# A hybrid decoder trunk on one core: the triangular solve of a gated DeltaNet layer is turned back one projection later

## Chip, core and metric

The kernel runs on one core of a Trainium2 chip. The metric is the device time of one execution in microseconds (us), the median of three runs. Five engines work side by side, each through its own instructions in order: TensorE (PE, matmuls and transposes), VectorE (DVE), ScalarE (ACT), GpSimd (POOL) and SyncE (SP, which here only issues DMAs).

## What is computed

Four pre-norm residual layers over 256 tokens of width 1024, in float32: a pooling mixer, a gated DeltaNet mixer (GDN), latent attention (MLA), and a pooling mixer again, then a final norm. Layer by layer it is

```python
h = rmsnorm(x, norm_g[i])
x = x + mixer(h)                     # pool, GDN, MLA, pool
```

The change lies mostly in the GDN layer. For 8 heads it projects `h` to q, k, v and a gate, runs a causal convolution of width 4 and a SiLU over q, k and v, and then needs the inverse of a unit lower triangular matrix per head and chunk:

```python
qkv = jax.nn.silu(causal_depthwise_conv(qkv, conv_w))
L = jnp.where(strict, jnp.einsum('bhnid,bhnjd->bhnij', k_beta, k) * decay, 0.0)
A = jnp.eye(C, dtype=L.dtype) + L
sol = lax.linalg.triangular_solve(A, rhs, left_side=True, lower=True)
```

`decay` is `exp(g_i - g_j)`; q and k are L2-normalised; the state is carried over the chunks, and the result is normalised, gated and projected out.

## The kernel before

**Weights.** Every weight comes as a strip `raw` of float32 (SP issues its DMA, L133). ACT rounds it to `whi` (L149, or L153 with a gain), and DVE takes the rest, `wlo = raw - whi` (L150, L154); for strips whose number stands in the argument `pool`, POOL does it. PE then adds three products per block, hTh·whi, hTl·whi and hTh·wlo (L162). `whi` and `wlo` have rings of 9 buffers, so ACT and DVE can be some strips ahead of PE and no further.

**The GDN layer** is written as a list of steps (the string `order`). `g0` to `g3` project the gate (and end in the SiLU `gsg`, L676); `k0 k1`, `q0 q1` and `v0` to `v2` each project 512 columns, run the convolution (ACT scales the first tap into `cv` or `vc`, L753; DVE adds three more, L756) and the SiLU (`kqT` L798, `vc` L920). k and q then go through PE transposes (L804), squares and sums for the norm (`sq`, `ssq`), and a product with kT (L817); v goes through transposes (L924) and a scaled copy (`vR`, L927). `V3` is the projection of v3 alone, `c3` the rest of it. `d` takes the exponentials of the decays `DT` and `Gb` on ACT (L746); `a0 a1` make the matrices `LT`.

**The solve.** `s` is a substitution over 32x32 blocks: DVE transposes them into `Lb` (L857), POOL runs 31 pairs of a multiplication and a subtraction (L863, L867), and the result is turned back by a DVE transpose (L869) and copied into `T` by ACT (L876) and by POOL (L878). `i` (inverses) joins the blocks to full inverses: transposes into `U` on DVE (L947), then matmuls in pairs (L956). `u0 u1` use them.

**Order.** The program is written straight on, and a scheduler then sorts each engine's instructions by when they can be ready; a `with later(...)` block keeps its instructions behind the ones that it names. Each engine runs its list strictly in that order. The steps stood as `g0 k0 d a0 g1 k1 a1 s q0 v0 v1 i v2 q1 V3 c3 g2 u0 u1 g3`, and turning back (L869 to L878) was the end of `s`, with nothing to hold it back.

**The norm.** `x` has two tiles of 128 tokens. Each finished part of the residual is squared and summed on ACT (`part_done`, L256), the sums are joined on POOL, and the last part reads the square root of what came before as an extra column of `x`, so that the sum over it is whole (L294, L297, L298). `begin` multiplies the first 256 columns of each half by the gain on POOL (`hg`, L385); `rest` raises to the power -1/2 (`xr`, L390) and makes `h` on DVE (L397) and ACT (L402).

Of the kernel before, what the change touches and what calls it, by code (L numbers as in the profile page):

```python
# [16 lines left out]
P = 128  # L17
# [25 lines left out]
def trunk(ctx: ExitStack, tc: tile.TileContext, x, positions, norm_g, pool_w_in, pool_w_grp,  # L43
# [241 lines left out]
    def part_done(t, a, n, apart=False):  # L285
        s = small(f"ms{t}{a // 256}", 1)
        end = a + n == D
        more = int(end and not apart)
        with later(*[m for e, m in mark.items() if e == "rest"]):
            sumsq(xs[t][:, a:a + n + more], n + more, s, scale=float(D) ** -0.5)  # L290
        if a == 0:
            nc.gpsimd.tensor_scalar(s, s, EPS, None, ALU.add)
        elif not more:
            nc.gpsimd.tensor_tensor(out=s, in0=s, in1=ms[t], op=ALU.add)  # L294
        ms[t] = s
        if a and not end:
            nc.gpsimd.tensor_scalar(s, s, float(D), None, ALU.mult)  # L297
            nc.gpsimd.tensor_tensor(out=xs[t][:, D:], in0=s, in1=half, op=ALU.pow)  # L298
# [5 lines left out]
    def load_x(t, c):  # L304
        sl = slice(c * CW, (c + 1) * CW)
        for b in range(2):
            nc.sync.dma_start(out=xs[t][b * 64:(b + 1) * 64, sl], in_=by_row(x, t)[b, :, sl])
# [3 lines left out]
    nc.scalar.dma_start(out=grow, in_=norm_g[0].rearrange("(k p) -> k p", p=P))  # L311
    ones = const.tile([P, P], F32, name="ones")
# [120 lines left out]
    class Final(Normed):  # L433
# [3 lines left out]
        def feed(self, t):  # L437
            y = self.rest(t) if final else [xs[t][:, :CW], xs[t][:, CW:D]]
            for c in range(2):
                sl = slice(c * CW, (c + 1) * CW)  # L440
                for b in range(2):
                    nc.sync.dma_start(out=by_row(out, t)[b, :, sl],
                                      in_=y[c][b * 64:(b + 1) * 64])

    def layer_out(w, yT, ks, i, gain=None):
# [62 lines left out]
    def pool_layer(i, j, hT):  # L508
# [80 lines left out]
        for g in order:  # L589
            gs = gate(g)  # L590
            if not place:
                with later(*[m for k, m in mark.items() if k not in ("rest", "strip")]):
                    turn_params()
                    window_counts()
            elif setups:
                with later(*[m for k, m in mark.items() if k not in ("rest", "strip")]):
                    setups.pop(0)()
# [57 lines left out]
    def gdn_layer(i, j, hT):  # L655
# [23 lines left out]
        order = "g0 k0 d a0 g1 k1 a1 s q0 v0 v1 i v2 q1 V3 c3 g2 u0 u1 g3".split()  # L679
# [63 lines left out]
        def decays():  # L743
            with later(mark["gate"]):
# [3 lines left out]
        def conv(*tiles):  # L748
# [5 lines left out]
            for ps, c, o in tiles:  # L754
                for d in range(1, 4):
                    nc.vector.scalar_tensor_tensor(out=o[:, d:], in0=ps[:, :S - d],  # L756
                                                   scalar=tp(3 - d, c), in1=o[:, d:],
                                                   op0=ALU.mult, op1=ALU.add)
# [4 lines left out]
        solve = big("solve", 2, B, C)  # L763
# [5 lines left out]
        Lg = small("Lg", M, B, bufs=1)  # L769
# [84 lines left out]
        def substitution():  # L854

            Lb = big("Lb", B, B)
            nc.vector.transpose(Lb, Lg.rearrange("p m c -> p c m")[:, :, None, :].to_broadcast(  # L857
                [P, B, 2, M]))
            pr = small("pr", 136, bufs=1)
# [569 lines left out]
```

## Time and profile before

| | |
|---|---|
| median of 3 runs | 821.5 us (821.17 to 821.84) |
| profiled execution | 820.01 us, span of its trace 818.3 us |
| PE busy in the span | 793.2 us, 97% |
| DVE / ACT / POOL busy | 599.4 / 499.8 / 144.9 us |
| HBM read | 136.74 MB |

All times below are counted from the start of the span. A row of the timeline has a start, a duration, the engine, the line, the operation with its output and inputs, and in brackets how long the engine stood idle before it and what ended that. A matmul's duration overlaps its neighbours', so what a matmul costs PE is the distance between two starts.

### The profile page before, as it was taken

What the parts mean: (1) busy time and instruction counts of PE and PEld (TensorE: products, weight loads), DVE (VectorE), ACT (ScalarE), POOL (GpSimd) and SP (SyncE); (2) the same over time, 40 slices, a digit from 0 to 9 for tenths busy, and PEclk for the clock granted to TensorE, in tenths of its full rate; (3) what the DMA queues carried; (4) which work ended last, traced back from release to release, by engine and by line L of the source; (5) the groups of instructions that cost most, each with busy time, mean ns of one, the idle gap of its engine ahead of it and who ended that gap; (6) DMA issues with size and microseconds to landing.
All of it is one profiled execution on the core that took longest, in us unless ns stands there. A gap on an engine that the chain in (4) does not pass through costs nothing.

```text
span 818.3 us, 16144 instructions
## 1 busy us (share of the span) xinstructions
PE 793.2 (97%) x5966; PEld 754.2 (92%) x5966; DVE 599.4 (73%) x1133; ACT 499.8 (61%) x1007; POOL 144.9 (18%) x300
## 2 busy tenths in 40 slices
PE   8999999999999699999999999999999999999996
PEld 7989998989999698888989999999999989999996
DVE  4699987566999586556677659778877668877862
ACT  5666665567967566456565655566565576566662
POOL 2001100234227821022212013000000210000012
PEclk9999999999999989999999999999999999999999
DMA  6765666646555343322557776753542546576562
GB/s 202 221 186 175 204 208 232 205 155 202 186 180 175 111 129 104 129 78 104 180 151 225 213 175 187 209 144 86 183 170 76 183 153 209 192 216 199 198 201 52
DMA packets 106615, 138.85 MB, mean 170 GB/s; under 512 B 19044, under 2 KB 48936, under 8 KB 106536
## 3 DMA queue, kind: packets, MB, share of 16 engines
q1 hardware_dynamic: 104352, 136.60, 54.3%
q0 software_dynamic: 320, 1.06, 0.4%
q8 instruction: 47, 0.77, 0.4%
q10 hardware_dynamic: 1864, 0.17, 0.2%
q14 instruction: 32, 0.26, 0.1%
HBM read 136.74 MB, written 1.06 MB: 168 GB/s over the span
## 4 chain that ended last, share of the span: by engine, by line
PE 83%; POOL 5%; DVE 5%; issue 2%; ACT 2%; DMA 2%; SPq 0%; POOLq 0%; ACTq 0%; DVEq 0%
PE acc L162 67%; PE aux L162 8%; POOL solve L867 2%; POOL pr L863 2%; DVE wlo L150 1%; DVE cv L756 1%; DVE h L397 1%; PE tp L1332 1%; DMA x<-in_x_dram 1%; DMA raw<-in_pool_w_in_dram 1%; ACT whi L149 0%; DMA raw<-in_gdn_w_in_dram 0%; PE aux L974 0%; PE tp L1070 0%; PE aux L817 0%
## 5 line engine op out<-in xcount | busy, mean ns | idle before, releaser
L150 DVE TENSOR_TENSOR wlo<-raw,whi 128x512 fp32r<-128x512 f32 (+1 forms) x372 | 252.1, 702 | 100.6 <-ACT whi L149 98.8
L149 ACT CAST whi<-raw 128x512 fp32r<-128x512 f32 (+1 forms) x380 | 224.7, 617 | 147.0 <-PE acc L162 81.0
L162 PE MATMUL acc<-hTh,whi 128*128 128x256 f32 x832 | 230.2, 277 | 1.2 <-ACT gsg L676 1.2
L162 PE MATMUL acc<-hTl,whi 128*128 128x256 f32 x832 | 230.9, 278 | 0.0
L162 PE MATMUL acc<-hTh,wlo 128*128 128x256 f32 x832 | 229.8, 277 | 0.0
L162 PEld LDWEIGHTS acc<-hTh,whi 128*128 128x128 f32 x832 | 160.6, 193 | 1.6 <-ACT gsg L676 1.4
L162 PEld LDWEIGHTS acc<-hTl,whi 128*128 128x128 f32 x832 | 160.6, 193 | 0.2
L162 PEld LDWEIGHTS acc<-hTh,wlo 128*128 128x128 f32 x832 | 160.4, 193 | 0.2
L162 PE MATMUL acc<-whi,yTh 128*128 128x256 f32 (+1 forms) x384 | 112.3, 315 | 0.0
L162 PE MATMUL acc<-wlo,yTh 128*128 128x256 f32 (+1 forms) x384 | 112.3, 311 | 0.0
L162 PE MATMUL acc<-whi,yTl 128*128 128x256 f32 (+1 forms) x384 | 89.1, 313 | 0.0
L162 PEld LDWEIGHTS acc<-wlo,yTh 128*128 128x128 f32 x384 | 73.2, 191 | 3.1
L162 PEld LDWEIGHTS acc<-whi,yTh 128*128 128x128 f32 x384 | 72.9, 191 | 3.1
L162 PEld LDWEIGHTS acc<-whi,yTl 128*128 128x128 f32 x384 | 63.1, 191 | 3.4
L153 ACT ACTIVATE whi<-raw,colsT 128x512 fp32r<-128x512 f32 x64 | 44.1, 720 | 30.1 <-DMA raw<-in_pool_w_out_dram 16.9
L153 ACT ACTIVATE whi<-raw,gain 128x512 fp32r<-128x512 f32 x64 | 43.8, 720 | 30.6 <-DMA raw<-in_pool_w_in_dram 25.8
L154 DVE SCALAR_TENSOR_TENSOR wlo<-raw,colsT,whi 128x512 fp32r<-128x512 f32 x64 | 47.3, 764 | 19.1 <-ACT whi L153 18.8
L385 POOL TENSOR_TENSOR hg<-x,gain 128x256 f32<-128x256 f32 x16 | 13.8, 872 | 242.6 <-DVE x L450 211.6
L162 PE MATMUL acc<-wlo,hTh 128*128 128x512 f32 (+1 forms) x144 | 54.7, 384 | 1.7 <-DVE wlo L150 1.5
L162 PE MATMUL acc<-whi,hTh 128*128 128x512 f32 (+1 forms) x144 | 53.0, 381 | 0.7 <-ACT hTh L242 0.7
L154 DVE SCALAR_TENSOR_TENSOR wlo<-raw,gain,whi 128x512 fp32r<-128x512 f32 x64 | 46.5, 745 | 9.8 <-ACT whi L153 9.4
L162 PE MATMUL acc<-whi,hTl 128*128 128x512 f32 (+1 forms) x144 | 42.2, 373 | 0.0
(370 smaller groups left out, 1509.9 us busy)
## 6 DMA issues: line engine op xcount, KB each, us to landing
raw<-in_pool_w_in_dram SPq DMA_DIRECT2D x62, 512.0 KB, 4.4
raw<-in_gdn_w_in_dram SPq DMA_DIRECT2D x48, 512.0 KB, 3.9
raw<-in_pool_w_out_dram SPq DMA_DIRECT2D x32, 512.0 KB, 4.3
raw<-in_mla_w_in_dram SPq DMA_DIRECT2D x24, 512.0 KB, 4.5
raw<-in_mla_w_uq_dram SPq DMA_DIRECT2D x36, 256.0 KB, 3.5
raw<-in_pool_w_grp_dram SPq DMA_DIRECT2D x16, 512.0 KB, 4.1
raw<-in_gdn_w_out_dram SPq DMA_DIRECT2D x16, 512.0 KB, 3.4
raw<-in_mla_w_ukv_dram SPq DMA_DIRECT2D x32, 256.0 KB, 3.5
```

The source lines that it names most:

```text
L149: a = nc.scalar.copy(hi, v)
L150: b = e.tensor_tensor(out=lo, in0=v, in1=hi.bitcast(F32), op=ALU.subtract)
L153: a = nc.scalar.activation(hi, v, AF.Copy, scale=g)
L154: b = e.scalar_tensor_tensor(out=lo, in0=v, scalar=g, in1=hi.bitcast(F32), op0=ALU.mult, op1=ALU.subtract)
L162: return nc.tensor.matmul(inorder(o, n), lhsT=lhs, rhs=woven(rhs, n), start=start, stop=stop)
L385: nc.gpsimd.tensor_tensor(out=self.early[t, a], in0=xs[t][:, sl], in1=self.g[:, sl], op=ALU.mult)
L397: nc.vector.scalar_tensor_tensor(out=h[:, cut:], in0=xs[t][:, sl], scalar=r[:, 0:1], in1=self.g[:, sl], op0=ALU.mult, op1=ALU.mult)
L756: nc.vector.scalar_tensor_tensor(out=o[:, d:], in0=ps[:, :S - d], scalar=tp(3 - d, c), in1=o[:, d:], op0=ALU.mult, op1=ALU.add)
L863: nc.gpsimd.tensor_tensor(out=pv, op=ALU.mult, in0=Lb[:, r + 1:, r:r + 1].to_broadcast([P, n, c]), in1=Tb[:, r:r + 1, :c].to_broadcast([P, ...
L867: mark["blocks"] = nc.gpsimd.tensor_tensor(out=tv, in0=tv, in1=pv, op=ALU.subtract).ins
L1332: nc.tensor.transpose(ps[:, a * P:(a + 1) * P], sb[:, a * P:(a + 1) * P], ident)
```

## The change

1. The steps are now `g0 k0 d a0 k1 a1 s g1 q0 v0 v1 v2 b q1 i V3 c3 g2 u0 u1 g3`: the projection `g1` goes from before `k1` to behind the start of the solve, turning back becomes a step `b` of its own behind `v2`, and `i` goes behind `q1`. `b` is kept behind the latest weight strip and the latest convolution.
2. The solve's buffers are no tiles of their own now: `Lb` lies in `U[0]`, the solution in `U[1]`, `Lg` and the products in the first `X1`. The two small operations on `rki` and `neG` stay in `s`; the multiplication of `ktok` goes with `b`.
3. The multiplication of `Gb` with q (`ev`) goes from POOL to DVE, out of the block that kept it behind the solve; POOL takes the strips (0, 4), none, (3, 7), (3, 7) of the four gate projections, where it took (0, 4), (7), none, (7).
4. The first `x` loads (columns 0 to 511) have their second half of the tokens issued by ACT, and those of tile 1 are issued right behind tile 0's; the last stores of tile 1 likewise go half by ACT.
5. In the norm, a factor D is folded into the scale of the sum, so the scalar multiplication at L297 goes; `hg` of the second half is put behind the power that follows.

```diff
-            sumsq(xs[t][:, a:a + n + more], n + more, s, scale=float(D) ** -0.5)
+            sumsq(xs[t][:, a:a + n + more], n + more, s, scale=unit ** 0.5)
...
-            nc.gpsimd.tensor_scalar(s, s, float(D), None, ALU.mult)
-            nc.gpsimd.tensor_tensor(out=xs[t][:, D:], in0=s, in1=half, op=ALU.pow)
+            mark["sofar"] = nc.gpsimd.tensor_tensor(out=xs[t][:, D:], in0=s, in1=half,
+                                                    op=ALU.pow).ins
...
-        for b in range(2):
-            nc.sync.dma_start(out=xs[t][b * 64:(b + 1) * 64, sl], in_=by_row(x, t)[b, :, sl])
+        for b, queue in enumerate((nc.sync, nc.scalar if c == 0 else nc.sync)):
+            queue.dma_start(out=xs[t][b * 64:(b + 1) * 64, sl], in_=by_row(x, t)[b, :, sl])
...
-                for b in range(2):
-                    nc.sync.dma_start(out=by_row(out, t)[b, :, sl],
-                                      in_=y[c][b * 64:(b + 1) * 64])
+                for b, queue in enumerate((nc.sync, nc.scalar if t else nc.sync)):
+                    queue.dma_start(out=by_row(out, t)[b, :, sl], in_=y[c][b * 64:(b + 1) * 64])
...
             if c == 0:
-                nxt.begin(t, CW)
+                with later(mark.pop("sofar")):
+                    nxt.begin(t, CW)
...
-                            pool=((0, 4), (7,), (), (7,))[vi])
+                            pool=((0, 4), (), (3, 7), (3, 7))[vi])
...
-        order = "g0 k0 d a0 g1 k1 a1 s q0 v0 v1 i v2 q1 V3 c3 g2 u0 u1 g3".split()
+        order = "g0 k0 d a0 k1 a1 s g1 q0 v0 v1 v2 b q1 i V3 c3 g2 u0 u1 g3".split()
...
-        solve = big("solve", 2, B, C)
+        U = [big("U", H, P) for _ in range(NT)]
+        Lb = U[0].rearrange("p m c -> p (m c)").rearrange("p (a b) -> p a b", a=B)
+        solve = U[1].rearrange("p m c -> p (m c)").rearrange("p (n a b) -> p n a b", n=2, a=B)
...
+            nc.vector.reciprocal(rki, rk)
+            nc.vector.tensor_scalar(neG, eG[:, 1, :], -1.0, None, ALU.mult)
+
+        def blocks_back():
+
             nc.vector.transpose(turned_.rearrange("p r c -> p (r c)"),
                                 Tb.rearrange("p r c -> p c r"))
...
+            nc.vector.tensor_tensor(out=ev, in0=ev, in1=qT[hf][:, :, P:], op=ALU.mult)
             with later(mark["blocks"]):
-                nc.gpsimd.tensor_tensor(out=ev, in0=ev, in1=qT[hf][:, :, P:], op=ALU.mult)
...
-            if name == "i":
-
-                with later(mark["strip"], mark["dve"]):
-                    inverses()
+            if name in "bi":
+
+                with later(mark["strip"], mark["dve" if name == "i" else "conv"]):
+                    once[name]()
...
-    load_x(1, 0)
```

How the lists of the engines change at three places; a row is one instruction, or several alike with their count.

ACT's list where step `k0` ends, before: the SiLU of k0 (`kqT`), the exponentials of the decays (`DT`, `Gb`), and the squares and copies of k0.

```order
L798 ACT_TABLE_LOAD
L798 ACTIVATE kqT<-cv 128x256 x4
L149 CAST whi<-raw 128x512
L746 ACT_TABLE_LOAD
L746 ACTIVATE DT<-DT 128x1024
L149 CAST whi<-raw 128x512 x2
L807 ACTIVATE sq<-tp 128x512
L810 COPY ktok<-tp 128x256
L807 ACTIVATE sq<-tp 128x512
L810 COPY ktok<-tp 128x256
L746 ACTIVATE DT<-DT 128x1024
L746 ACTIVATE Gb<-Gb 128x1024
```

The same place on ACT in the changed kernel (its lines are some numbers higher).

```order
L804 ACT_TABLE_LOAD
L804 ACTIVATE kqT<-cv 128x256 x3
L748 ACT_TABLE_LOAD
L748 ACTIVATE DT<-DT 128x1024
L149 CAST whi<-raw 128x512
L804 ACT_TABLE_LOAD
L804 ACTIVATE kqT<-cv 128x256
L149 CAST whi<-raw 128x512 x2
L748 ACT_TABLE_LOAD
L748 ACTIVATE DT<-DT 128x1024
L748 ACTIVATE Gb<-Gb 128x1024
L813 ACTIVATE sq<-tp 128x512
```

The first exponential now stands between the third and the fourth SiLU, with two more table loads around it, and the squares stand behind all three exponentials.

DVE's list where the solve is turned back, before: convolutions of v1 (`vc`), then the transpose, then the last convolutions of v1 and strips.

```order
L150 TENSOR_TENSOR wlo<-raw,whi 128x512
L756 SCALAR_TENSOR_TENSOR vc<-acc,tap,vc 128x254
L869 STREAM_TRANSPOSE solve<-solve 128x512
L756 SCALAR_TENSOR_TENSOR vc<-acc,tap,vc 128x253
L150 TENSOR_TENSOR wlo<-raw,whi 128x512
L756 SCALAR_TENSOR_TENSOR vc<-acc,tap,vc 128x253
L150 TENSOR_TENSOR wlo<-raw,whi 128x512 x3
L756 SCALAR_TENSOR_TENSOR cv<-acc,tap,cv 128x255
```

The same place on DVE in the changed kernel: the `vc` ahead of the transpose are now those of v2, and the `cv` behind it those of q1.

```order
L758 SCALAR_TENSOR_TENSOR vc<-acc,tap,vc 128x254
L150 TENSOR_TENSOR wlo<-raw,whi 128x512
L758 SCALAR_TENSOR_TENSOR vc<-acc,tap,vc 128x253
L878 STREAM_TRANSPOSE U<-U 128x512
L758 SCALAR_TENSOR_TENSOR cv<-acc,tap,cv 128x255
L150 TENSOR_TENSOR wlo<-raw,whi 128x512 x2
L758 SCALAR_TENSOR_TENSOR cv<-acc,tap,cv 128x254
L758 SCALAR_TENSOR_TENSOR cv<-acc,tap,cv 128x253
L758 SCALAR_TENSOR_TENSOR cv<-acc,tap,cv 128x255
```

The transpose moved behind the last convolution of one more projection; what stands right behind it is q1's.

ACT's list at the copies out of the turned solution, before: the copies into `T`, and behind them the SiLU of v1.

```order
L927 ACTIVATE vR<-tp,rki 128x256 x4
L149 CAST whi<-raw 128x512 x2
L876 COPY T<-solve 32x16x32 x2
L920 ACTIVATE vc<-vc 128x512
L149 CAST whi<-raw 128x512
L920 ACTIVATE vc<-vc 128x512
```

And in the changed kernel.

```order
L927 ACTIVATE vc<-vc 128x512
L755 ACTIVATE cv<-acc,tap 128x256 x2
L149 CAST whi<-raw 128x512 x2
L927 ACTIVATE vc<-vc 128x512
L885 COPY T<-U 32x16x32 x2
L934 ACTIVATE vR<-tp,rki 128x256 x2
L755 ACTIVATE cv<-acc,tap 128x256
L149 CAST whi<-raw 128x512 x2
L804 ACTIVATE kqT<-cv 128x256
```

No SiLU of a v projection stands behind the copies now; the next thing of PE's that depends on a row behind them is the convolution and the SiLU of q1.

More of the change, by code (lines that the diff above doesn't have):

```diff
@@ L288, in part_done @@
         more = int(end and not apart)
+        unit = 1.0 / D if end or apart else 1.0
         with later(*[m for e, m in mark.items() if e == "rest"]):
-            sumsq(xs[t][:, a:a + n + more], n + more, s, scale=float(D) ** -0.5)
+            sumsq(xs[t][:, a:a + n + more], n + more, s, scale=unit ** 0.5)
         if a == 0:
-            nc.gpsimd.tensor_scalar(s, s, EPS, None, ALU.add)
+            nc.gpsimd.tensor_scalar(s, s, EPS * D * unit, None, ALU.add)
         elif not more:
@@ L591, in pool_layer @@
             if not place:
-                with later(*[m for k, m in mark.items() if k not in ("rest", "strip")]):
+                with later(*[m for k, m in mark.items() if k not in ("rest", "strip", "conv")]):
                     turn_params()
@@ L595, in pool_layer @@
             elif setups:
-                with later(*[m for k, m in mark.items() if k not in ("rest", "strip")]):
+                with later(*[m for k, m in mark.items() if k not in ("rest", "strip", "conv")]):
                     setups.pop(0)()
@@ L743, in decays @@
         def decays():
-            with later(mark["gate"]):
+            with later(*[m for n, m in mark.items() if n == "gate"]):
                 for a in (*DT, Eb, eG):
@@ L755, in conv @@
                 for d in range(1, 4):
[L756 to L758 removed]
+                    mark["conv"] = nc.vector.scalar_tensor_tensor(
+                        out=o[:, d:], in0=ps[:, :S - d], scalar=tp(3 - d, c), in1=o[:, d:],
+                        op0=ALU.mult, op1=ALU.add).ins
         Q, B = 4, 32
         C = B // 2
[L763 removed]
+        U = [big("U", H, P) for _ in range(NT)]
+        Lb = U[0].rearrange("p m c -> p (m c)").rearrange("p (a b) -> p a b", a=B)
+        solve = U[1].rearrange("p m c -> p (m c)").rearrange("p (n a b) -> p n a b", n=2, a=B)
         Tb, turned_ = solve[:, 0], solve[:, 1]
@@ L768, in gdn_layer @@
                                   which[:, a, :C])
-        Lg = small("Lg", M, B, bufs=1)
+        X1 = [big("X1", H, P)]
+        LX = X1[0].rearrange("p m c -> p (m c)")
+        Lg = LX[:, :M * B].rearrange("p (m c) -> p m c", m=M)
         Ts = big("T", NT, H, P)
@@ L854, in substitution @@
         def substitution():
-            Lb = big("Lb", B, B)
             nc.vector.transpose(Lb, Lg.rearrange("p m c -> p c m")[:, :, None, :].to_broadcast(
                 [P, B, 2, M]))
-            pr = small("pr", 136, bufs=1)
+            pr = LX[:, M * B:]
             for r in range(B - 1):
@@ L932, in values @@
             values_done(vi)
-        U = []
         u1 = []
         def inverses():
-            U.extend(big("U", H, P) for _ in range(NT))
-            X1 = [big("X1", H, P) for _ in range(NT)]
+            X1.append(big("X1", H, P))
             for t in range(NT):
@@ L1006, in gdn_layer @@
                  "c": values_done}
-        once = {"s": substitution, "d": decays, "i": inverses}
+        once = {"s": substitution, "d": decays, "b": blocks_back, "i": inverses}
         for name in order:
-            if name == "i":
-                with later(mark["strip"], mark["dve"]):
-                    inverses()
+            if name in "bi":
+                with later(mark["strip"], mark["dve" if name == "i" else "conv"]):
+                    once[name]()
             elif name in once:
```

5 lines of the change are left out of this document (2 added, 3 removed).

## The prediction

> **What bounds the kernel now.** I read the page first (busy shares), then the list of PE's waits, then the timeline around the longest of them.
>
> ```profile
> PE 793.2 (97%) x5966; PEld 754.2 (92%) x5966; DVE 599.4 (73%) x1133; ACT 499.8 (61%) x1007; POOL 144.9 (18%) x300
> ...
> PE tp L924 <- ACT vc L920: 7.8, 1, 7.8
> PE tp L359 <- DMA x<-in_x_dram: 2.6, 2, 2.2
> ...
> PE acc L162 <- DVE wlo L150: 1.5, 3, 0.8
> PE acc L162 <- ACT gsg L676: 1.2, 1, 1.2
> ```
>
> PE is busy 793.2 of 818.3 us, so at most 25.1 us can come from its idle time. One wait, 7.8 us long, holds a third of that: PE wants to transpose v1's `vc` and ACT has not written it. The timeline says why. The rows are of ACT, DVE, POOL and PE.
>
> ```profile
> 284.01 2.14 ACT L876 COPY T<-solve 32x512 f32<-32x512 f32 x2 [9.08 <-DVE solve L869]
> 286.18 0.63 ACT L920 ACTIVATE vc<-vc 128x512 f32<-128x512 f32 x1
> ...
> 274.45 0.47 DVE L756 SCALAR_TENSOR_TENSOR vc<-acc,tap,vc 128x254 f32<-128x254 f32 x1
> 282.94 1.04 DVE L869 STREAM_TRANSPOSE solve<-solve 128x512 f32<-128x512 f32 x1 [8.01 <-POOL solve L867]
> ...
> 282.68 0.22 POOL L867 TENSOR_TENSOR solve<-solve,pr 128x16 f32<-128x16 f32 x1
> 282.86 1.27 POOL L896 TENSOR_TENSOR Gb<-Gb,kqT 128x512 f32<-128x512 f32 x1
> ...
> 286.42 2.55 POOL L878 COPY T<-solve 32x512 f32<-32x512 f32 x2
> ...
> 286.86 1.11 PE L924 MATMUL tp<-ident,vc 128*128 128x128 f32 x4 [7.79 <-ACT vc L920]
> ...
> 293.02 1.90 PE L956 MATMUL aux<-T,LT 128*128 128x64 f32 x16
> ```
>
> Read upwards: PE waits for a SiLU that waits in ACT's list behind the copies into `T`; these wait for DVE's transpose, which has stood 8.01 us, since 274.92, for POOL's substitution. v1's last convolutions are queued behind that transpose. It is an order problem, not a shortage of any engine. The gap costs more than its length; the table by stretches (PE's count of matmuls in it, then its granted clock) shows what follows:
>
> ```profile
> 240.00:270.00 30.00, 30.00 (x272) 30.00 (x271) 30.00 (x63) 23.12 (x50) 21.14 (x40) 1.00 0.61 178
> ...
> 287.00:292.00 5.00, 5.00 (x24) 5.00 (x25) 4.30 (x6) 5.00 (x13) 2.92 (x5) 0.50 0.61 161
> 292.00:293.00 1.00, 1.00 (x8) 1.00 (x7) 1.00 (x2) 0.78 (x2) 0.00 (x0) 0.66 0.64 246
> ```
>
> The columns behind the length are PE, PEld, DVE, ACT and POOL. At full clock PE starts 272 matmuls in 30 us, 0.110 us each. Right after the gap the clock is 0.50 and 24 take 5.00 us where 2.65 would do, then 8 take 1.00 where 0.88 would do: 2.5 us more. The gap's price is 7.79 + 2.5 = **10.3 us**.
>
> **The change, part by part.**
>
> *Turning back one projection later: -10.3.* A projection of a v is 96 matmuls, 96 x 0.110 = 10.6 us. Before the transpose DVE's list now holds v2's convolutions as well, so DVE gets there some 10.6 us later than 274.9, at about 285.5. When does the substitution end? POOL finished it at 282.90. Its start can move: `g1` is now behind it, which takes 10.6 us of PE's work from ahead of it, but what starts it is DVE, and DVE is 30.00 of 30.00 us busy in the stretch above, so it works off a backlog; I take 1.5 us earlier of the possible 10. Its length can grow: all 31 pairs ran from 247.7 on, and the last 20 rows of them (the two groups of 275 to 283) while DVE stood idle.
>
> ```profile
> L863 POOL TENSOR_TENSOR pr<-Lb,solve x31: 215/408/907, 247.7 to 282.4; 128x126 f32<-128x126 f32 x3, 128x30 f32<-128x30 f32 x2, 128x56 f32<-128x56 f32 x2, 128x78 f32<-128x78 f32 x2
> ...
> L867 POOL TENSOR_TENSOR solve<-solve,pr 128x110 f32<-128x110 f32 (+9 forms) x10 | 3.3, 326 | 0.7
> L863 POOL TENSOR_TENSOR pr<-Lb,solve 128x110 f32<-128x110 f32 (+9 forms) x10 | 3.1, 312 | 0.8
> ...
> 270.49 0.43 POOL L863 TENSOR_TENSOR pr<-Lb,solve 128x130 f32<-128x130 f32 x1
> 271.52 0.91 POOL L863 TENSOR_TENSOR pr<-Lb,solve 128x120 f32<-128x120 f32 x1
> ```
>
> Beside a busy DVE the same kind of row takes 0.43 or 0.91 us, about the size or twice it. So these 6.4 us become 6.4 to 12.8, and the end lies between 281.4 and 287.8 against DVE's arrival at 285.5: DVE waits 0 to 2.3 us, where it waited 8.01. A v projection's SiLU no longer stands behind it. **What is late next** is what PE reads of the solve: the pairs of the inverses need both copies into `T`. Behind the solve's end these took until 288.97, 6.1 us, of which 1.3 us was the `Gb` product (now on DVE); so 4.8 us behind the later of the solve's end and DVE's arrival: 290.3 to 292.6. PE came to its pairs at 293.02, without the gap at 282.7, in the midst of v2; now they stand behind q1's projection and within V3's, while `g1` and the rest ahead of them stay, so half a projection later: 288.0, an estimate. That is a new wait of 2.3 to 4.6 us; I take **2.3**, because DVE's arrival is the firmer of the two numbers, with 0 and 6 as bounds. The stretch with the 1.2 us wait for `gsg` shows no lower clock, so nothing is added for a wait not much longer:
>
> ```profile
> 206.00:220.00 14.00, 12.84 (x115) 12.65 (x114) 12.93 (x34) 13.41 (x24) 5.26 (x6) 1.00 0.54 163
> ```
>
> *k0 and the decays on ACT: +1.6.* This is the part that costs.
>
> ```profile
> 202.59 1.28 ACT L798 ACT_TABLE_LOAD   x1
> 203.88 1.34 ACT L798 ACTIVATE kqT<-cv 128x256 f32<-128x256 f32 x4
> 205.13 0.60 ACT L149 CAST whi<-raw 128x512 fp32r<-128x512 f32 x1
> ...
> 207.04 1.07 ACT L746 ACTIVATE DT<-DT 128x1024 f32<-128x1024 f32 x1
> ```
>
> The fourth SiLU now has two table loads, an exponential and a strip ahead of it: 2 x 1.28 + 1.07 + 0.60 = 4.2 us later. PE needs it for its transposes, but has matmuls of the next projection to do meanwhile; the bounds are 0 and 4.2. The nearest row is PE's wait for `gsg`, where one table load ahead of a SiLU cost PE 1.2 us; I take 1.6, a little more. The squares stand behind the two other exponentials, so `ssq` is late by about 3 us on DVE; this is DVE's and POOL's time, which delays the start of the solve, and is why I gave that only 1.5 us there.
>
> The page "ScalarE: Activation LUTs" of the Trainium skill, section "What ACT_TABLE_LOAD costs", says that each switch of tables costs a drain of about 1.38 us besides the load, 2.66 us in all. Here the first load ends at 203.87 and the next instruction starts at 203.88, so the trace does not show the drain. By the page the fourth SiLU would be 2.8 us later still and the sum 2.8 us worse.
>
> *`gsg`: -1.2.* PE's wait of 1.2 us for `gsg` came from a table load ahead of the SiLU of `g1`; behind `k1` the table is already the right one. The load itself moves ahead of k1's first SiLU, where it is paid at 0 to 1.3 us; I count the bound and not the value.
>
> *Products and strips.* `ev` took 1.27 us on POOL (row above), twice; on DVE I take it as no longer, hidden behind the up to nine strips that PE has ahead of it: nothing, or 2.5 us without that cover. The two more strips that POOL makes, of the same size, come at `g2` and `g3`, behind the same ring of nine: nothing, or again 2.5 us. The buffers inside `U` and `X1` add no instruction; what they delay (the second `X1` zeroed) is off PE's path.
>
> *First loads: -0.6.*
>
> ```profile
> 0.80 1.21 SPq L307 DMA_DIRECT2D x<-in_x_dram  x2
> 2.05 0.59 SPq L133 DMA_DIRECT2D raw<-in_pool_w_in_dram  x1
> 2.68 1.11 SPq L307 DMA_DIRECT2D x<-in_x_dram  x2
> ...
> 8.38 1.09 PE L359 MATMUL tp<-ident,x 128*128 128x128 f32 x4 [2.19 <-DMA x<-in_x_dram]
> ```
>
> SP needs about 0.6 us per issue, and one issue less stands ahead of the first strip and of tile 1's first half. Tile 1's second half goes from ACT, behind `grow` and a table load, at about 3.4, no earlier than before (3.3). PE's second wait lasts until these bytes are there; I take one issue, 0.6 us, with 0 and 1.2 as bounds.
>
> *The end: -1.1.*
>
> ```profile
> 809.25 6.24 SPq L442 DMA_DIRECT2D out_dram<-h  x7
> 809.49 0.73 POOL L385 TENSOR_TENSOR hg<-x,gain 128x256 f32<-128x256 f32 x1 [1.39 <-DVE x L450]
> 810.18 0.19 POOL L294 TENSOR_TENSOR ms<-ms,ms 128x1 f32<-128x1 f32 x1
> 810.44 0.42 DVE L450 TENSOR_TENSOR x<-acc,x 128x256 f32<-128x256 f32 x1 [1.09 <-PE acc L162]
> 810.46 0.23 POOL L297 TENSOR_SCALAR ms<-ms 128x1 f32<-128x1 f32 x1
> 810.77 0.57 POOL L298 TENSOR_TENSOR x<-ms,half 128x1 f32<-128x1 f32 x1
> 811.37 0.42 ACT L256 ACTIVATE junk<-x 128x257 f32<-128x257 f32 x1 [1.42 <-POOL x L298]
> 811.96 0.55 POOL L390 TENSOR_TENSOR xr<-ms,neghalf 128x1 f32<-128x1 f32 x1 [0.62 <-ACT junk L256]
> 812.54 0.95 ACT L402 ACTIVATE h<-hg,xr 128x256 f32<-128x256 f32 x2 [0.66 <-POOL xr L390]
> ```
>
> ACT's last sum starts at 811.37, 0.5 us behind DVE's last `x` (810.86), because POOL did `hg` and the scalar first. Without these the power is done by 810.85, and ACT starts at about 810.9; then `xr` waits a little for `hg`, which is now in between (until about 811.6): 0.36 us. The four stores of tile 1 start from 813.0 to 814.9 on one queue. On two, ACT cannot issue before its own `h` ends at 813.49, so its second starts near 814.1: 0.75 us. Together 1.1, bounds 0.3 and 1.6.
>
> *The shorter norm at the three borders between layers: -0.6.* There PE waits for `wlo` 1.5 us in all (row above); each border can gain 0.36 us, and not all of it is on the path. Bounds 0 and 1.1.
>
> **The sum.** -10.3 + 2.3 + 1.6 - 1.2 - 0.6 - 1.1 - 0.6 = -9.9 us. Against the profiled execution's own 820.0 us that is 810.1; the median of the runs lies 1.5 us above that execution, so I forecast **811.6 us**. With all bounds at their better end it is -15.4, without the new waits, and some 17 if the other small waits of the layer go too; with all at their worse, -10.3 + 6 + 4.2 + 1.3 + 2.5 + 2.5 - 0.3 = +5.9.
>
> **Rivals.**
>
> *The wait only moves.* The substitution is not finished when DVE gets there, and the pairs, or q1's SiLU behind the copies on ACT, take the gap's place. For it: POOL's chain is 35 us long and starts only 1.5 us earlier in my reading. Against it: 8.0 us of waiting, plus a projection's 10.6 us, is more than the 6.4 us by which the chain can grow. It would leave a wait of 5 us in place of 2.3, and the half clock behind it, 2.5 us: the gain falls to 9.9 - 5.2 = 4.7, so 816.8. The clock decides part of this. The trace shows a half clock after 7.79 us of idling and none after 1.2. The page "TensorE: Matmul & The Clock Gate" of the Trainium skill, section "HAM oscillation — how this bites in real kernels", sets the limit at an idle time of about 3.4 us; by it a wait of 3 us would go without the 2.5 us.
>
> *Slower: ACT and DVE become the bound between k0 and the solve.* k0 and k1 now follow each other, with 13 table loads in place of 11, and what used to be spread over `g1` is pressed together. If PE waits the full 4.2 us at k0, 1.3 at k1's load, and the substitution starts no earlier and takes the full 6.4 us more, DVE waits 4 us with q1's convolutions and V3's strips behind it and PE about 6 us with its 2.5 us of half clock: 4.2 + 1.3 + 6 + 2.5 = 14.0 us of new waits against 11.5 removed, so +2.5; with start, end and borders worth nothing that is 824.0. It is slower than before from new waits of 11.5 us on in that case, of 13.8 us on with start, end and borders as in the sum. Against it: DVE idles while it waits, and then POOL's rows are short, which limits the wait by itself.
>
> *Start and end are hidden.* Tile 1's first half is issued by 3.8 and used at 8.38, so bytes and not issues may hold it back; and the last store may wait for its landing whichever queue it is on. Then 1.7 us of the sum go: 813.3.
>
> **How the numbers follow.** The forecast as stated has a chance of 0.58, start and end hidden 0.15, the moved wait 0.20, slower 0.07. Up to 0.2% (1.6 us, about what a measurement of this kernel can tell from no change) I count as the same: a third of the worst part of the moved wait, 0.05. That gives faster 0.88, same 0.05, slower 0.07. The range goes from 805.0 (all small waits gone) to 817.5, beyond the moved wait at 816.8.
>
> **What would show it.** In the changed profile: no PE wait on `vc` (L927); the granted clock at 1.00 through 280 to 300; DVE's transpose (L878) with less than 3 us of idling ahead of it; PE's waits in the layer at k0's transposes (L810) and at the pairs (L961), 1 to 3 us each; DVE still full between 240 and 280; POOL's last solve row between 281 and 288, shifted by what the start gains; the last store issued near 805. The forecast is wrong if a PE wait of more than 3 us stands at L961 or at q1's transposes, if PE stands 3 us or more at L810, or if the layer's first half (to the start of the substitution) takes longer than before.

## The result, and the profile after

| | before | changed |
|---|---|---|
| median of 4 runs, side by side | 821.67 us (821.17 to 822.87) | 817.08 us (816.5 to 817.17) |
| ratio of the runs | | 0.9926 (0.9898 to 0.9954) |
| span of the profiled execution | 818.3 us | 815.4 us |
| layer: from the transpose of `G` to the first product with the state | 149.6 us | 149.5 us |

The change gains 4.6 us by the medians and 2.9 us by the two profiles, where 9.9 were forecast. The last row is the difference of two starts on PE: the transpose of `G` (194.1 before, 193.4 now) and the first L1033, now L1038 (343.7 and 342.9). It holds everything that was done to the solve, and it is as long as before. Both profiles are single executions; the two of the changed kernel (this one and that of e5_changed_again below) differ by 1.9 us in this stretch. Behind it they do not: from the first product with the state to the end of the span it takes 474.6 us before and 472.5 in both profiles of the changed kernel.

PE's waits in the changed kernel's whole span (total, times, longest):

```profile
PE 794.6 (97%) x5966; PEld 754.8 (93%) x5966; DVE 598.6 (73%) x1133; ACT 500.2 (61%) x1009; POOL 148.7 (18%) x292
...
PE tp L810 <- ACT kqT L804: 7.2, 3, 3.4
PE acc L162 <- ACT ph L242: 2.8, 1, 2.8
...
PE acc L162 <- DVE wlo L150: 0.2, 1, 0.2
```

The wait for `vc` is gone, and so are that for `gsg` and most of that for `wlo`. In their place PE waits three times for the SiLU of a k or q projection. (The wait for `ph` stands at 57 us, in the first layer, where no step was moved; over all the traces it varies from 1.5 to 3.5 us.) The timeline of PE gives the places, k0, k1 and q1, and the stretches behind the last two show the clock:

```profile
209.84 0.44 PE L810 MATMUL tp<-ident,kqT 128*128 128x128 f32 x2 [1.26 <-ACT kqT L804]
...
228.58 0.69 PE L810 MATMUL tp<-ident,kqT 128*128 128x128 f32 x2 [3.35 <-ACT kqT L804]
...
294.78 0.44 PE L810 MATMUL tp<-ident,kqT 128*128 128x128 f32 x2 [2.63 <-ACT kqT L804]
...
228.00:230.00 2.00, 1.42 (x7) 1.43 (x8) 1.29 (x4) 1.99 (x7) 0.00 (x0) 0.62 0.64 225
...
297.00:298.00 1.00, 1.00 (x6) 1.00 (x6) 1.00 (x3) 0.64 (x2) 0.00 (x0) 0.50 0.53 137
```

Taking busy time times what is missing of the clock, over stretches of 2 us, the lower clock costs 2.9 us in the layer before and 3.2 us now. With the waits that is 7.8 + 1.2 + 2.9 = 11.9 us lost before and 7.2 + 3.2 = 10.4 now. The other 1.4 us by which the layer should then be shorter are not found in these rows.

**Why k1 waits 3.35 us.** Read these from the bottom, on ACT, SP and DVE of the changed kernel:

```profile
214.65 1.45 DVE L814 TENSOR_REDUCE ssq<-sq 128x4 f32<-128x512 f32 x2 [3.03 <-ACT sq L813]
216.41 2.17 DVE L758 SCALAR_TENSOR_TENSOR cv<-acc,tap,cv 128x255 f32<-128x255 f32 x5 [0.32 <-ACT cv L755]
218.50 0.68 DVE L150 TENSOR_TENSOR wlo<-raw,whi 128x512 fp32r<-128x512 f32 x1
...
219.21 0.37 SPq L133 DMA_DIRECT2D raw<-in_gdn_w_in_dram  x1
...
222.98 1.15 ACT L149 CAST whi<-raw 128x512 fp32r<-128x512 f32 x2 [3.29 <-DMA raw<-in_gdn_w_in_dram]
225.66 1.14 ACT L149 CAST whi<-raw 128x512 fp32r<-128x512 f32 x2 [1.53 <-DMA raw<-in_gdn_w_in_dram]
226.81 1.28 ACT L804 ACT_TABLE_LOAD   x1
228.11 1.03 ACT L804 ACTIVATE kqT<-cv 128x256 f32<-128x256 f32 x3
```

ACT has the strips ahead of k1's SiLU in its list, and these had not landed. SP could issue the strip only at 219.21, when a `raw` buffer came free; before, the corresponding issue was at 214.41:

```profile
214.41 0.37 SPq L133 DMA_DIRECT2D raw<-in_gdn_w_in_dram  x1
```

The buffer was held by `wlo` (218.50), which stood in DVE's list behind the sum of k0's squares, and that waited 3.03 us for squares which ACT makes behind three exponentials and their table load. This chain is read from the rows; which of its links a run bears out is said at e3_decays_late.

**Why q1 waits.** The substitution on POOL, then DVE, then ACT:

```profile
L867 POOL TENSOR_TENSOR X<-U x31: 216/433/1538, 248.7 to 288.3; 128x126 f32<-128x126 f32 x3, 128x30 f32<-128x30 f32 x2, 128x56 f32<-128x56 f32 x2, 128x78 f32<-128x78 f32 x2
...
288.84 1.07 DVE L878 STREAM_TRANSPOSE U<-U 128x512 f32<-128x512 f32 x1 [3.85 <-POOL U L871]
...
289.94 2.21 ACT L885 COPY T<-U 32x512 f32<-32x512 f32 x2 [3.62 <-DVE U L878]
292.16 0.84 ACT L934 ACTIVATE vR<-tp,rki 128x256 f32<-128x256 f32 x2
292.89 0.47 ACT L755 ACTIVATE cv<-acc,tap 128x256 f32<-128x256 f32 x1
293.25 1.14 ACT L149 CAST whi<-raw 128x512 fp32r<-128x512 f32 x2
294.27 0.45 ACT L804 ACTIVATE kqT<-cv 128x256 f32<-128x256 f32 x1
```

The substitution starts 1.0 us later than before, not earlier, and takes 40.1 us where it took 35.2. DVE and ACT both stand at the turning back, and q1's SiLU is behind it in ACT's list as v1's was.

### The profile page after: what moved, and what is told of

It is laid out like the page before. It is cut to its first block, busy times and chain, and to the rows that moved or that the text cites. A ratio compares the mean times of both kernels' runs of the same rounds, so it can differ in the third digit from the quotient of the medians.

```text
span 815.4 us, 16122 instructions
## 1 busy us (share of the span) xinstructions
PE 794.6 (97%) x5966; PEld 754.8 (93%) x5966; DVE 598.6 (73%) x1133; ACT 500.2 (61%) x1009; POOL 148.7 (18%) x292
## 4 chain that ended last, share of the span: by engine, by line
PE 85%; POOL 5%; ACT 3%; DVE 3%; issue 2%; DMA 1%; ACTq 0%; SPq 0%; DVEq 0%; POOLq 0%
PE acc L162 69%; PE aux L162 8%; POOL X L867 2%; POOL U L871 2%; ACT whi L149 1%; PE tp L1337 1%; DVE cv L758 1%; DMA x<-in_x_dram 1%; DVE wlo L150 1%; PE aux L823 1%; ACT junk L256 1%; PE tp L419 0%; PE aux L979 0%; PE aux L961 0%; PE aux L1002 0%
```

## The experiments

Theory A, as formed from these rows: the layer gives back at k0, k1 and q1 what the gap cost, by the two chains above; the rest of the gain is the loads, the stores and the norm. Every group of runs was timed beside the kernel before. "Layer" is measured as in the table above; a profile of one execution scatters there by about 2 us. "Border" is what a later section explains.

| run | median | before beside it | ratio (95%) | layer | border |
|---|---|---|---|---|---|
| e1_turn_only | 823.75 | 822.8 | 1.0019 (1.0001 to 1.0036) | 150.6 | late |
| e2_g1_only | 825.83 | 822.8 | 1.0043 (1.0025 to 1.0062) | 155.3 | early |
| e3_decays_late | 821.64 | 822.8 | 0.9992 (0.9977 to 1.0007) | 149.9 | late |
| e4_edges | 821.57 | 822.8 | 0.9995 (0.9975 to 1.0016) | 147.5 | late |
| e5_changed_again | 818.47 | 822.81 | 0.9949 (0.9928 to 0.9971) | 151.4 | early |
| e6_turn_after_q1 | 819.29 | 822.81 | 0.9952 (0.9936 to 0.9968) | 152.0 | early |
| e7_turn_after_q1_g1_back | 819.38 | 822.81 | 0.9959 (0.9944 to 0.9974) | 145.8 | late |
| e8_both | 815.28 | 822.81 | 0.9905 (0.9885 to 0.9926) | 146.6 | early |
| e9_layer_alone | 822.06 | 824.58 | 0.9981 (0.9964 to 0.9998) | 148.6 | early |
| e10_turn_alone | 824.97 | 824.58 | 1.0008 (0.9992 to 1.0024) | 151.1 | early |
| e11_decays_old_norm | 822.79 | 824.58 | 0.9983 (0.9968 to 0.9998) | 154.7 | early |
| e12_g1_back_old_split | 811.48 | 824.58 | 0.9844 (0.9819 to 0.9869) | 143.0 | early |

### The two moves apart

e1_turn_only, against the changed kernel:

```diff
-        order = "g0 k0 d a0 k1 a1 s g1 q0 v0 v1 v2 b q1 i V3 c3 g2 u0 u1 g3".split()
+        order = "g0 k0 d a0 g1 k1 a1 s q0 v0 v1 v2 b q1 i V3 c3 g2 u0 u1 g3".split()
```

> The changed kernel with g1 put back between a0 and k1; turning back stays behind v2 (order g0 k0 d a0 g1 k1 a1 s q0 v0 v1 v2 b q1 i V3 c3 g2 u0 u1 g3). Theory A (moving g1 is what gives the gain back: k1 right behind k0 meets ACT's exponentials and late strips): the waits at k0 and k1 (1.3 and 3.4 us, and 1.5 us of lower clock behind the second) go, the wait of q1 (2.6 us) stays or grows by 1 to 3, so 3 to 6 us faster than the changed kernel, about 812. Rival B (the late turning itself only moves the wait): PE's wait at q1 grows by what the substitution starts later, 4 us or more, and the time is that of the changed kernel or above, 816 to 819.

e2_g1_only (`b` there without its `later`):

```diff
+        order = "g0 k0 d a0 k1 a1 s b g1 q0 v0 v1 i v2 q1 V3 c3 g2 u0 u1 g3".split()
```

> The changed kernel with the turning back right behind the substitution and the inverses behind v1, as before; only g1 stands behind the substitution (order g0 k0 d a0 k1 a1 s b g1 q0 v0 v1 i v2 q1 V3 c3 g2 u0 u1 g3). Theory A: the waits at k0 and k1 stay as in the changed kernel (1.3 and 3.4 us) and the old gap behind the solve is still there, shorter by what the substitution starts earlier at most; so slower than the changed kernel by 3 to 8 us, 820 to 825. Rival B (the earlier start of the substitution is what helps): the gap falls under 3 us and the time is within 2 us of the changed kernel.

The waits of e1, then of e2, on PE:

```profile
219.97 0.38 PE L162 MATMUL acc<-hTh,whi 128*128 128x256 f32 x1 [1.56 <-ACT gsg L678]
...
295.93 0.69 PE L810 MATMUL tp<-ident,kqT 128*128 128x128 f32 x2 [5.72 <-ACT kqT L804]
```

```profile
228.91 0.69 PE L810 MATMUL tp<-ident,kqT 128*128 128x128 f32 x2 [3.57 <-ACT kqT L804]
...
289.09 1.12 PE L931 MATMUL tp<-ident,vc 128*128 128x128 f32 x4 [6.15 <-ACT vc L927]
```

With g1 back, k0's and k1's waits vanish as theory A has it, but q1's grows by 3.1 us, just beyond A's 1 to 3 and short of rival B's 4 or more. Neither had the time: 823.75 us is 12 above A's 812 and 5 above B's upper end. B's reason is not there either: the substitution starts 54.7 us after G's transpose, 55.3 in the changed kernel. What lengthens the wait at q1 is shown at e11 below, and part of the time is lost at the border. With g1 moved alone, k1's wait is there and the old gap too, 6.2 us: A was right, with a time just above its range. Neither move alone is worth anything; together they only just are.

### k0's exponentials

e3_decays_late:

```diff
-            with later(*[m for n, m in mark.items() if n == "gate"]):
-                for a in (*DT, Eb, eG):
+            for a in (*DT, Eb, eG):
+                with later(mark["gate"], mark["silu" if a is DT[0] else "ktok"]):
                     nc.scalar.activation(a, G if a is eG else a, AF.Exp)
```

> The changed kernel, with the first exponential of the decays kept behind the fourth SiLU of k0, and the others behind k0's squares and copies. Theory A (split table loads and squares behind the exponentials make DVE idle for 3.0 us, so the strips of k1 are freed, issued and landed some 5 us late, and k1's SiLU waits behind them on ACT): PE's wait at k0 goes, that at k1 falls from 3.4 us to 1 or less with no lower clock behind it; 4 to 6 us faster than the changed kernel, 811 to 813. Rival B (with k1 right behind k0 the strips are late in any case): DVE does not idle but the strips still land late, PE's wait at k1 stays above 2 us, and at most 2 us are won.

The rows of PE and one of ACT:

```profile
208.86 0.44 PE L810 MATMUL tp<-ident,kqT 128*128 128x128 f32 x2 [0.47 <-ACT kqT L804]
...
221.02 0.44 PE L810 MATMUL tp<-ident,kqT 128*128 128x128 f32 x2 [1.69 <-ACT kqT L804]
...
294.08 0.69 PE L810 MATMUL tp<-ident,kqT 128*128 128x128 f32 x2 [2.59 <-ACT kqT L804]
...
219.26 1.28 ACT L804 ACT_TABLE_LOAD   x1
```

k0's wait falls to 0.5 us and k1's from 3.4 to 1.7, without a lower clock behind it; the 1.7 are near the length of the table load that is left there. What this bears out is the last link of the chain: the scheduler put four strips ahead of k1's first SiLU where there were nine, and the SiLU no longer stands behind the late one. That strip itself is no earlier: it is issued 26.8 us after G's transpose, 25.8 in the changed kernel, while DVE now waits 1.55 us for the last exponential (`eG`). In the runs with g1 back in its place the strip at the same place in the queue is issued at 19.8 to 20.9, as before (20.3). So that the strips are late because the squares are late is read from the rows and not shown by a run. The time is not what A gave: by the ratios the kernel was 3.5 us slower than the changed one (0.9992 against 0.9949 in e5), which led to the border and to e11.

### The edges alone

e4_edges is the kernel before with parts 4 and 5 of the change, as in its diff above; among them

```diff
+        for b, queue in enumerate((nc.sync, nc.scalar if c == 0 else nc.sync)):
...
+                with later(mark.pop("sofar")):
+                    nxt.begin(t, CW)
```

> The kernel before with the first loads, the last stores and the shorter norm alone (parts 4 and 5 of the change). Theory A (the whole net gain of the changed kernel, some 2.9 us by the profiles, comes from these and the GDN layer as a whole gains nothing): 2.5 to 3.5 us faster than before, about as fast as the changed kernel. Rival B (part of the gain is the layer's): 1.5 us or less.

1.2 us by the medians, which is in rival B's range. But its layer happened to take 147.5 us, and behind the layer it takes 475.8 us where the changed kernel takes 472.5: 3.3 us are lost, at the border below. So this run does not decide.

### Again the changed kernel

No edit.

> The changed kernel as it is, beside runs of the kernel before that spread by several us (in the last four comparisons from 818.0 to 827.1). Theory A (the layer gains nothing net, only the first loads, the last stores and the norm do): 1 to 3.5 us faster than before, as e4_edges within 1.5 us. Rival B (the 4.6 us of the first comparison are the change's): 4 to 5.5 us faster.

4.3 us, as the first time: B. The gain is real. With e9 below its parts can be told.

### Turning back behind q1

e6 and e7 put `b` behind q1 and `i` behind V3; e7 has g1 where it was before; e8 is e6 with e3's decays.

```diff
+        order = "g0 k0 d a0 k1 a1 s g1 q0 v0 v1 v2 q1 b V3 i c3 g2 u0 u1 g3".split()   # e6, e8
+        order = "g0 k0 d a0 g1 k1 a1 s q0 v0 v1 v2 q1 b V3 i c3 g2 u0 u1 g3".split()   # e7, e12
```

> The changed kernel with the turning back put behind q1 and the inverses behind V3 (order ... v2 q1 b V3 i c3 g2 u0 u1 g3). Theory A (the wait that is left at the solve is q1's SiLU queued on ACT behind the copies into T, and q1's convolutions on DVE behind the transpose): PE's wait of 2.6 us for q1 and the lower clock behind it (some 2 us) go, unless the pairs of the inverses now wait; 3 to 5 us faster than the changed kernel. Rival B (the solve simply ends too late, whoever waits for it): a wait of 2 us or more appears at the pairs or at what follows them, and the time stays within 1.5 us of the changed kernel.

> As the kernel before, g1 between a0 and k1 as there, with the turning back behind q1 and the inverses behind V3 (and the other parts of the change). Theory A: neither the waits at k0 and k1 nor that of q1; PE's waits in the layer sum up to 3 us or less (10.1 in the profile before with the clock behind), so 6 to 9 us faster than before. Rival B: the substitution, which starts one projection later in PE's work, is late for the pairs: a wait of 4 us or more at them, and at most 3 us faster than before.

> The changed kernel's order with the turning back behind q1 (as e6) and the decays behind k0's SiLU and squares (as e3). Theory A: both remedies add up, PE's waits in the layer 3 us or less, 6 to 9 us faster than before and at least as fast as e7. Rival B (k0 and k1 back to back keep a wait of about 2 us at k1 whatever ACT's order is): 2 us slower than e7.

In none of the three does PE wait for q1 any more. e6 still gains nothing over the changed kernel, and PE's rows show where it is given back:

```profile
210.60 0.44 PE L810 MATMUL tp<-ident,kqT 128*128 128x128 f32 x2 [2.04 <-ACT kqT L804]
...
229.64 0.44 PE L810 MATMUL tp<-ident,kqT 128*128 128x128 f32 x2 [3.65 <-ACT kqT L804]
...
332.29 3.16 PE L979 MATMUL aux<-T,LT 64*128 64x64 f32 x16 [0.67 <-ACT T L976]
336.24 1.97 PE L985 MATMUL aux<-U,X 64*64 64x64 f32 x16 [0.79 <-DVE X L982]
338.14 6.17 PE L1002 MATMUL aux<-vR,U 128*128 128x256 f32 x16
```

k0 and k1 still cost 5.7 us and their clock, and the last step of the inverses now stands alone at 330 to 338, with no projection left to fill it, at half clock (e6, 336 to 338):

```profile
336.00:338.00 2.00, 1.76 (x16) 1.76 (x16) 0.18 (x1) 0.00 (x0) 0.00 (x0) 0.50 0.05 12
```

That is rival B's time, though no wait of 2 us: the two waits are 1.5 us together, and the half clock lasts 10.24 us. It is there in e7, e8 and e12 too, for 3.41 to 6.83 us, so turning back this late has a price of its own. e8, with k0 and k1 mended too, waits 2.3 us for k1's SiLU and 0.8 at the inverses, 3.1 in all where A put 3 or less, and is 7.5 us faster than before: A. The longest wait at k1, 1.7 us, is near the 2 us of its rival B, but not the time. e7's layer is as short as e8's, but its waits there sum up to 4.6 us where A put 3 or less, and it is 3.4 us faster than before where A put 6 to 9. Rival B's wait at the pairs is not there either.

### The border far away

The trace of e7 loses its gain at the border between MLA and the last layer, 300 us behind the edit. From the last MLA transpose (L1337) to the last transpose of the pooling layer's group (L585) e7 takes 84.3 us, e8 78.0; over the softmax stage ahead of it e7 takes 1.6 less, so it loses 4.7. (From the first product with the state to the end of the span it takes 477.1 us in e7, 475.8 to 477.0 in e1, e3 and e4, and 472.5 in e8.) The scheduler had placed strips there later: ACT's list has 2, 2, then 10 around the sums of squares in e1, e3, e4 and e7, and 4, 4, then 4 in all the others and in the kernel before. In e7, PE waits there for ACT's `h`:

```profile
PE tp L419 <- ACT h L404: 1.6, 1, 1.6
...
PE acc L162 <- ACT hTh L242: 1.2, 3, 0.7
```

This was found after e1 to e8 had run. The last four runs were chosen so that the border is the early one in all.

> The changed kernel with the first loads, the last stores and the norm as before, so the parts of the change in the GDN layer alone. Its strips at the border between MLA and the last layer are placed as in the kernel before and in the changed one (2, 4, 4 ahead of the sums). Theory A (the layer gives back at k0, k1 and q1 all that the gap cost): the layer takes 149 to 151 us from G's transpose to the first state product, as before, and the time is within 1.5 us of before. Rival B (the layer did gain, hidden by the scatter of single profiles): the time is 3 to 4.5 us below before, as the changed kernel.

> As e9_layer_alone, with g1 back between a0 and k1: the late turning alone. The border of the last layer is as in the kernel before here, where e1_turn_only had its strips placed later (2, 2, 2, then 10). Theory A (e1 was slower for two reasons: 3 to 5 us at that border, and a wait of 5 to 6 us at q1 in place of the old gap): within 1.5 us of before or up to 3 faster, so 3 us or more below e1's ratio; the wait at q1 is 5 to 6 us. Rival B (e1's time is the layer's): slower than before again, by 0.5 us or more.

> As e3_decays_late, with the norm as before, with which the strips at the border of the last layer are placed as in the changed kernel. Theory A (the remedy of the decays is worth 2 to 4 us in the layer, and e3 lost as much at the border): 5 to 7 us faster than before; waits at k0 and k1 2.5 us in all, that of q1 2.6 us with a lower clock behind it. Rival B (the remedy is worth nothing): as the changed kernel or slower, at most 4 us faster than before.

> As e7_turn_after_q1_g1_back, with POOL's strips of the gate projections as in the kernel before; with them the border of the last layer is placed as there. Theory A (the layer takes 146 us in this order, and e7 lost 4 to 5 us at the border): 7 to 9 us faster than before, as e8_both or better. Rival B (the border costs nothing and e7's time is its own): 3 to 5 us faster than before.

e9 undoes parts 4 and 5 of the change, e10 is e9 with e1's order, and e11 is e3 with the norm as before. In short, for the norm (e9, e10, e11), then for the loads and stores (e9, e10):

```diff
+            nc.gpsimd.tensor_scalar(s, s, float(D), None, ALU.mult)
...
-                with later(mark.pop("sofar")):
-                    nxt.begin(t, CW)
+                nxt.begin(t, CW)
...
-        for b, queue in enumerate((nc.sync, nc.scalar if c == 0 else nc.sync)):
+        for b, queue in enumerate((nc.sync, nc.sync)):
...
-                for b, queue in enumerate((nc.sync, nc.scalar if t else nc.sync)):
+                for b, queue in enumerate((nc.sync, nc.sync)):
```

e12 is e7 with

```diff
-                            pool=((0, 4), (), (3, 7), (3, 7))[vi])
+                            pool=((0, 4), (7,), (), (7,))[vi])
```

e9: the layer's parts alone are 0.19% faster than before (0.02 to 0.36), 1.6 us where the whole change has 4.2 in e5: between A's bound and B's, and nearer A. e10: the late turn alone gives 0.08% slower (0.08 faster to 0.24 slower), at q1 6.5 us:

```profile
299.44 0.69 PE L809 MATMUL tp<-ident,kqT 128*128 128x128 f32 x2 [6.52 <-ACT kqT L803]
```

The time is within A's 1.5 us of before, but only 0.1% (0.9 us) below e1's where A asked for 3 us, and the wait is above its 5 to 6. Rival B's 0.5 us lie within the interval too, so this run does not decide between them. e1 has parts 4 and 5 besides and the late border, and is 0.1% slower than e10; with 0.3% for parts 4 and 5 (e5 against e9: 0.9949 and 0.9981) the late border costs some 0.4%, 3.5 us, an estimate from ratios that are each uncertain by about 0.2%; the traces give 3.3 to 4.6 us (475.8 to 477.1 against 472.5). e11: theory A fell. It is 0.17% (1.4 us) faster than before where A put 5 to 7 us, which is rival B's range. PE's waits at k0 and k1 are 3.5 us in all (4.6 in the changed kernel, 2.2 in e3), but PE stands 7.3 us at q1; DVE, ACT and PE of e11:

```profile
291.13 1.08 DVE L878 STREAM_TRANSPOSE U<-U 128x512 f32<-128x512 f32 x1 [7.64 <-POOL U L871]
...
297.73 2.35 DVE L952 STREAM_TRANSPOSE U<-T 128x1024 f32<-128x1024 f32 x2
300.01 1.21 DVE L758 SCALAR_TENSOR_TENSOR cv<-acc,tap,cv 128x253 f32<-128x253 f32 x3
...
292.25 2.16 ACT L885 COPY T<-U 32x512 f32<-32x512 f32 x2 [7.76 <-DVE U L878]
...
300.54 0.44 ACT L804 ACTIVATE kqT<-cv 128x256 f32<-128x256 f32 x1 [0.50 <-DVE cv L758]
...
301.03 0.69 PE L810 MATMUL tp<-ident,kqT 128*128 128x128 f32 x2 [7.25 <-ACT kqT L804]
```

It is not that POOL's chain ends later. Counted from G's transpose, its first and its last multiplication start at 53.6 and 88.3 us before, at 55.3 and 94.9 in the changed kernel, at 53.9 and 90.9 in e3 and at 57.2 and 94.0 in e11. The difference is behind it: from the end of DVE's transpose to PE's first transpose of q1 it takes 8.8 us in e11 and e10, 8.0 in e1 and e3, and 4.9 in the changed kernel. In these four runs the scheduler put all four first taps of q1 behind the copies on ACT, where the changed kernel has two, and on DVE the transposes `U<-T` of `i` ahead of q1's last convolutions, for which the SiLU then waits. So 3 to 4 us of the wait at q1 in e1, e10 and e11 are this order and not the late turning as such.

e12 has the waits neither at k0 and k1 nor at q1: g1 in its old place, `b` behind q1, the old split. PE's waits of its whole span:

```profile
PE acc L162 <- ACT ph L242: 2.5, 1, 2.5
PE acc L162 <- ACT gsg L678: 2.1, 1, 2.1
...
PE aux L961 <- POOL T L887: 0.2, 1, 0.2
PE tp L810 <- ACT kqT L804: 0.2, 1, 0.2
```

Of the layer's long waits `gsg` is left, 2.1 us. POOL's last multiplication starts 94.4 us after G, hardly earlier than in the changed kernel, and PE waits no longer than 0.2 us for what POOL hands over. Rival B falls, and A's 7 to 9 us were too few: it is the fastest of all, 13.1 us below the kernel before beside it, 1.56% (1.31 to 1.81). Of the 1.15% between e7 and e12, some 9 us, the profiles show 4.7 at the border and 2.8 in the layer; the rest is not accounted for. The two profiles differ by 3.6 us in all (816.0 and 812.4), because e12's takes 3.8 us longer up to G's transpose. The split is the one thing edited between the two runs, so that the border is what it changes is read from the traces.

## Why the prediction was right in range and too high in gain

**The number and the signs.** The median of 817.08 us lies 0.4 inside the upper bound of 817.5, 5.5 above the forecast, and next to the rival "the wait only moves" (816.8), which the range was drawn to take in. That the rival's figure fits so well is partly luck: it put 5 us of waiting and 2.5 of lower clock at one place, and the runs have 2.6 and 1.7 at q1 and 3.4 and 1.5 at k1. Of the signs that the prediction named for being wrong, two came: PE stands 3.35 us at L810, and the layer's first half, up to the start of the substitution, takes 1.7 us longer. The sum at the worse bounds leaves out the 1.2 us gained at `gsg`; with them it is +4.7 and not +5.9.

**Right.** The gap at `vc` and its half clock went, 10.3 us, and so did the wait for `gsg`. k0's SiLU costs 1.3 us where 1.6 were put. The new wait at the solve is 2.6 us where 2.3 were put, but that agrees by accident: it is at q1's SiLU, and at the pairs PE waits for nothing. Start: PE's first products on tile 1 begin 1.0 us earlier (8.38 to 7.34) against 0.6, but this is not the new order of the loads: with the old one they begin at 7.07 in e9 and 7.79 in e10, with the new one at 7.62 in e5, so no gain is shown here. End: from DVE's last `x` to the end of the span it takes 7.0 us where it took 7.9, 0.9 against 1.1 (7.8 in e9 and e10, 7.0 in e5); ACT's sum now starts 0.1 us behind that `x`, and its second `h` waits 0.3 us for a store, which nobody had counted:

```profile
808.40 0.42 DVE L451 TENSOR_TENSOR x<-acc,x 128x256 f32<-128x256 f32 x1 [1.10 <-PE acc L162]
...
808.94 0.42 ACT L256 ACTIVATE junk<-x 128x257 f32<-128x257 f32 x1 [1.03 <-DVE x L451]
...
810.94 0.51 ACT L404 ACTIVATE h<-hg,xr 128x256 f32<-128x256 f32 x1 [0.32 <-DMA out_dram<-h]
```

Borders: PE's waits for `wlo` fell from 1.5 to 0.2 us, against 0.6 (1.4 in e9, 1.3 in e10, with the old norm). By the ratios parts 4 and 5 together are worth about 0.3% (e5 against e9), 2.6 us, against 2.3. Behind the layer the traces show 2.0 of it: 474.4 us in e9, 473.7 in e11, which has the new stores and the old norm, and 472.5 in the changed kernel. The rival that start and end are hidden is out for the end; for the start it stands.

**The steps that failed.** First, "I count the bound and not the value", on the table load that moves ahead of k1's first SiLU, together with the sentence before it that the late squares are "DVE's and POOL's time, which delays the start of the solve". By the rows they are also the strips' time: `wlo` stands in DVE's list behind the sum of squares, holds the `raw` buffer, and so the next strip lands late, on ACT ahead of k1's SiLU. The runs show that the wait comes with g1 behind k1 and goes with g1 back, and that it shrinks when the late strip no longer stands ahead of the SiLU; that the late squares delay the strip is not shown by a run. The wait is 3.35 us, and 1.5 us of lower clock behind it, where nothing was counted. The shape was in the lists of ACT and DVE; what was queued behind the waiting instruction on DVE was not followed to the buffer that it frees.

Second, the wait at the solve, put at "the pairs of the inverses" with "nothing is added for a wait not much longer". It is at q1's SiLU, which ACT's list ahead of the prediction already had behind the copies, and its 2.63 us were followed by 1.7 us of lower clock. The Trainium skill's rule against idle gaps of PE above some 3.4 us ("TensorE: Matmul & The Clock Gate", "HAM oscillation — how this bites in real kernels") would have let this wait pass as well; here the clock fell. Third, "1.5 us earlier" for the start of the substitution: it started 1.7 us later after G, and lengthened by 4.9 of the 6.4 us that were its bound. The rival "the wait only moves" was thus the nearer one in its mechanism, at two places.

**What does not follow.** The drain per table load that the prediction quotes from the Trainium skill ("ScalarE: Activation LUTs", "What ACT_TABLE_LOAD costs") is not seen in the changed kernel either: the load at 226.81 lasts 1.28 and `kqT` starts at 228.11. That the layer gains nothing at all is not shown: by the ratios its parts are worth 0.19% with an interval that nearly reaches nothing, by the profiles they vary from -1.0 to +1.8 us. The solve's new buffers (part 2) and the `ev` on DVE (part 3) stand in every run that has the layer's parts; none takes them out, so what they cost or gain is open.

## What to carry to other kernels

A wait that is an order problem moves with the order: when a slow chain on one engine ends in instructions on engines that run strictly in order, look for the last thing that needs it and put the hand-over behind everything that others need first. Here one projection later moved the wait from v1 to q1, and two projections later removed it, at the price of a lower clock at the last step of the inverses. When an instruction waits, follow what is queued behind it to the buffers that it frees, and those to the transfers that wait for them. With a scheduler that places by estimates, compare the whole order far from the edit too, before a time is put down to the edit. And where runs of one program scatter by several us, time the stages in the traces one by one: some agree to 0.1 us.

## What the runs showed of the hardware

The granted clock is not decided by the length of one wait. It stayed at 1.00 behind 2.76 us of idling in e10 (at 223.85) and fell behind 2.63 in the changed kernel, there only from 296.8 on, 2.0 us after PE had resumed. At one and the same place, PE's wait for `ph` in the first layer, it fell with 2.12 us in e7 and stayed at 1.00 with 2.17 in e5. In e7 it fell during a wait of 1.30 us, at 305.6:

```profile
304.00:306.00 2.00, 0.70 (x7) 0.56 (x7) 2.00 (x5) 0.63 (x1) 0.00 (x0) 0.89 0.66 152
306.00:308.00 2.00, 2.00 (x7) 1.80 (x8) 1.30 (x3) 1.47 (x3) 0.00 (x0) 0.50 0.96 348
```

In all fourteen traces, leaving out the first 14 and the last 10 us, a stretch at 0.50 lasts 3.41 us or two, three or four times that: 3.41 behind k1 and again behind q1 in the changed kernel, 10.24 at the gap in the kernel before, 13.65 in e11. So the lower clock is paid in steps, and one program pays at different places: e5's profile shows none behind a wait of 3.67 us at k1 and 6.83 us behind q1.

In e6 waits of 0.67 and 0.79 us among matmuls of 64x64 were enough (0.50 from 334 to 342), while the same step among wide matmuls in the kernel before kept 1.00 from 328 to 344. From the first to the last multiplication POOL's 31 pairs took 34.5 us in e10, where DVE idled 5.7 us at their end, and 41.0 in e6, where it never waited for them. And the scatter of one program was several times that of the first comparison: the kernel before ran from 818.0 to 827.2 us in the later groups. In the two profiles of the changed kernel it lies ahead of the state's first product: 193.4 and 195.0 us up to G's transpose, 149.5 and 151.4 in the layer, 472.5 in both behind it.
